# Rotary keys as the third column tile of w, and the early sums of w_out on ScalarE alone, in a hybrid attention block

## Chip, cores and metric

The kernel runs on one core of a Trainium2 chip. The metric is the device time in microseconds (us) of one execution; of the kernel before there are three timed runs and one more execution that was profiled. Engines are named TensorE (PE), VectorE (DVE), ScalarE (ACT), GpSimd (POOL) and SyncE (SP), as in the profile.

## The reference

One layer, 1024 tokens, width 1024, float32 in and out. One projection gives all heads; its columns are split among two head groups, and the result goes through the output projection and a layer norm:

```python
h = jnp.einsum('bsd,de->bse', x, w_in[layer])
q_a, k_a, v_a, z_a, q_b, k_b, v_b, z_b = jnp.split(h, SPLIT_POINTS, axis=-1)
y_a = neighborhood_attention(q_a..., k_a..., v_a..., rel_pos_bias[layer])   # 8 heads, 8 x 16 window of the grid
qb, kb = rotary(q_b..., positions), rotary(k_b..., positions)
y_b = windowed_gqa_with_sink(qb, kb, v_b..., sink_logits[layer])            # 8 query heads, 2 key heads
mixed = jnp.concatenate([y_a * silu(z_a), y_b * silu(z_b)], axis=-1)
y = jnp.einsum('bse,ed->bsd', mixed, w_out[layer])
x = layer_norm(DEEPNORM_ALPHA * x + y, ln_gain[layer], ln_bias[layer])
```

Rotary rotates each head of q_b and k_b by an angle that depends on the token; the keys k_b have 2 heads of 64, which is 128 columns of `w_in` and so one column tile of the kernel.

## The kernel before, in words

**Numbers.** Every float32 operand of a matmul is split into a high and a low float16 half, scaled by a power of two, and a product is three matmuls (high x high, high x low, low x high). ScalarE makes the high halves, GpSimd or VectorE the low ones.

**Stages.** First the values v are projected (line 537). Then come the 21 column tiles of `w_in` without v, 128 columns each, in the order of the list `ORDER` (lines 30 and 31): `zb` and `z` are gates of the two groups, `kb` and `qb` the rotary keys and queries, `k` and `q` those of the neighbourhood attention. The first six (`NPRO`) run ahead of the attention; the other fifteen (`FILL`) are pumped, matmul by matmul, between the steps of the attention. The attention has 128 units, one a step, group b first. The output projection and the layer norm end the kernel.

**A column tile** (`project`, lines 411 to 435) has two halves of 512 tokens; each half is 24 matmuls of 512 columns into one of two PSUM banks called `ps_pj`. Before a third half may start, the bank of the half two before it must have been emptied (`new_group`, line 406). Emptying is `evac`'s work:

- A gate tile named in `ORDER[:3]` is emptied by one Silu on ScalarE (line 391). A later gate tile takes a Tanh on ScalarE (line 394) and then a product on VectorE (line 395).
- A rotary tile (`rope`, line 358) is emptied by one scaled copy on ScalarE (line 364). Ahead of the attention VectorE then does a shuffle, two multiplications with cos and sin and an addition (lines 365 to 368); ScalarE casts the high halves (line 300, two instructions), VectorE subtracts to get the low ones (line 306, two), and for keys GpSimd copies both to the other 64 partitions (line 347, four).

**What sets the order.** From line 620 on the order of each engine's instructions is that in which the program emits them. Ahead of the attention a counter of matmuls (`ran`, 48 a tile) rules: an operation can be put at a count (`at`), or some matmuls after the end of a half. For a rotary tile the shuffle comes 2, the multiplications 3 and the addition 4 matmuls after the half's end, the casts 28, the subtractions 32, the copies 32 and 36 (lines 328 to 370).

Each tile needs a scale of its own, taken from sums of |w|: two sums on ScalarE (`w_scan`, line 260), one small matmul over all partitions (line 266) and five small VectorE instructions (lines 267 to 271), put 18 matmuls into the second half of the tile two before. All of `FILL` shares one scale. Its fifteen sums (`sum_w`, line 749: 12 on ScalarE at line 755, 3 on VectorE) are spread over counts 14 to 210; each has its own load of 512 KB (`ws`, line 689) on SP's queue. The last two, sums 13 and 14, sit at count 194, and the small matmul that adds them up on TensorE stands at count 217 (line 770), 25 matmuls later. Sixteen small VectorE instructions follow it (lines 267 to 286).

SP's queue also holds the loads of w's halves (line 229), each of which waits until GpSimd has made the low half five before it (line 246, lines 254 and 255), and the stores of v (line 739). What stands behind a waiting load waits too.

**The attention's planner.** During the attention a planner (lines 147 to 221 and 1379 to 1468) counts what it has given to each engine (`due`), with costs written down by hand, against 1.88 us a step (`at_step`). Work with a fixed engine is popped from queues; work that is not urgent goes by `fill_in` to an engine whose account has room (`ROOM`) before the next step, and work marked "any" to whichever asks first among those in its `cost`. Such are the sums of |w_out|, 16 of them (`wo_scan`, line 964): ScalarE (line 968) or VectorE (line 970) adds up one 128 x 512 piece. Four are made before the attention, on ScalarE. Twelve are created at the steps of `SCAN_LD` (0, 2, 4, 6, 8, 10, 13 and so on), together with their loads; each runs when its load is in, some steps later. The load of a piece waits for the sum four before it. When all 16 are made, the scale of `w_out` is worked out (line 782) and its split begins.

Of the kernel before, what the change touches and what calls it, by code (L numbers as in the profile page):

```python
# [26 lines left out]
QSCALE = 2.0 ** -15  # L27
LTT, LPP, BH, ND, NA, NX, F1 = 1, 6, 9, 1, 1, 8, 0.2
NSPLIT, NP = 6, 2
ORDER = ["zb0", "z0", "zb1", "kb", "qb0", "z1", "qb1", "zb2", "qb2", "k0", "qb3", "zb3", "q0", "k1", "q1",  # L30
         "k2", "q2", "k3", "q3", "z2", "z3"]
NPRO = 6
NS = 21 - NPRO
NR = 5
FILL = ORDER[NPRO:]
FILL_AT = [0, 8, 17, 25, 33, 41, 49, 57, 66, 74, 82, 90, 98, 106, 113, 121, 123.5, 126, 128, 131, 136]
# [29 lines left out]
def hybrid_block(ctx, tc, xT, x, wt, wv, wo, bias, sink, gain, lbias, cos, sin, bmask, out):  # L66
# [33 lines left out]
    def zslot(name, tag="z"):  # L100
        return zp.tile([128, S], F32, tag=tag, name=name, bufs=3 if tag == "z" else 1)
# [15 lines left out]
    invt = const.tile([128, 2], F32, name="invt")  # L117
    NT = len(ORDER)
    unit = const.tile([128, 2], F32, name="unit")
# [29 lines left out]
    clock = {"step": None}  # L149
# [19 lines left out]
    def enq(eng, fn, *deps, prio=1, after=0, cost=None):  # L169
        op = Op(eng, fn, deps, prio, cost)  # L170
        if clock["step"] is not None:
            queues[eng].append(op)
        elif after:
            events.setdefault(ran[0] + after, []).append(op.emit)
        else:
            op.emit()
        return op
# [44 lines left out]

    NH = 2 * len(ORDER)
    NL = NH - 2 * NR
# [37 lines left out]
    def w_scale(n):  # L262
# [8 lines left out]
        nc.vector.tensor_scalar(v, g, xrs, 0.5, op0=ALU.mult, op1=ALU.mult)  # L271
        nk, nq = ORDER.index("kb"), ORDER.index("qb0")
        if n >= NPRO - 1:
# [44 lines left out]
    def split_q(p, half, src, dep=None):  # L318
        col = dep is None
        ops, high = [], []  # L320
        prio = 0 if dep is None else 1
        eng = "pool" if dep and clock["step"] is not None else "dve"
        for j in range(2):
            a, o = slice(64 * j, 64 * j + 64), slice(64 - 64 * j, 128 - 64 * j)
            hi, lo = split_hl(lambda j=j, a=a: place(own("q", p, j), a, half, col),
                              lambda j=j, o=o: place(own("q", p, j), o, half, col),
                              taken_from(src, a, col), dep is None, eng)
            high.append((enq("act", hi, dep, prio=prio, after=28 if dep else 0), lo))
        for j, (o1, lo) in enumerate(high):
            ops.append(enq(eng, lo, *([o1] if dep else [h[0] for h in high]), prio=prio, after=32 if dep else 0))  # L330
            stk_ops.setdefault((p, j, half), []).append(ops[-1])
        return ops

    def split_k(p, half, src, dep=None):
        col = dep is None
        ops, high = [], []
        prio = 0 if dep is None else 1
        eng = "pool" if dep and clock["step"] is not None else "dve"
        for j in range(2):
            a, o = slice(64 * j, 64 * j + 64), slice(64 - 64 * j, 128 - 64 * j)  # L340
            hi, lo = split_hl(lambda j=j, a=a: place(own("kh", p, j), a, half, col),
                              lambda j=j, a=a: place(own("kl", p, j), a, half, col),
                              taken_from(src, a, col), dep is None, eng)

            def dup_(w, j=j, a=a, o=o):
                t = own(w, p, j)
                nc.gpsimd.tensor_copy(place(t, o, half, col), place(t, a, half, col))  # L347

            high.append((enq("act", hi, dep, prio=prio, after=28 if dep else 0), lo, dup_))
        for j, (o1, lo, dup_) in enumerate(high):  # L350
            o2 = enq(eng, lo, *([o1] if dep else [h[0] for h in high]), prio=prio, after=32 if dep else 0)
            ops.append(o2)
            dup = [enq("pool", lambda d=dup_: d("kh"), o1, after=32 if dep else 0, cost=0.62),
                   enq("pool", lambda d=dup_: d("kl"), o2, after=36 if dep else 0, cost=0.62)]
            stk_ops.setdefault((p, j, half), []).extend(dup)
        return ops

    def rope(ps, half):
        live = clock["step"] is not None
        sl = slice(512 * half, 512 * half + 512)  # L360
        eng, mul = ("pool", nc.gpsimd) if live else ("dve", nc.vector)
        raw = tiles["ap"].tile([128, 1024], F32, tag="va", name="rp_raw", bufs=6)[:, :512]
        sw = tiles["ap"].tile([128, 1024], F32, tag="va", name="rp_sw", bufs=6)[:, :512]
        o1 = enq("act", lambda: nc.scalar.activation(raw, ps, AF.Copy, scale=QSCALE), prio=0)
        o2 = enq("dve", lambda: nc.vector.stream_shuffle(sw, raw, SWAP), o1, after=2)
        o3 = enq(eng, lambda: mul.tensor_mul(raw, raw, tiles["cos"][:, sl]), o2, after=3)
        o4 = enq(eng, lambda: mul.tensor_mul(sw, sw, tiles["sin"][:, sl]), o2, after=3)
        o5 = enq(eng, lambda: mul.tensor_add(raw, raw, sw), o3, o4, after=4)
        return raw, o1, o5

    def evac(name, half, ps):
        sl = slice(512 * half, 512 * half + 512)
        kind = name.rstrip("0123")
        p = int(name[-1]) if name[-1].isdigit() else 0
        n = ORDER.index(name)
        if kind in ("kb", "qb"):
            raw, o1, o5 = rope(ps, half)
            if kind == "kb":
                split_k("b", half, raw, o5)
            else:  # L380
                split_q(f"b{p}", half, raw, o5)
            return [o1]
        if kind == "k":
            return split_k(p, half, ps)
        if kind == "q":
            return split_q(p, half, ps)
        e = 4 + p if kind == "zb" else p
        if half == 0:
            zt[e] = zslot(f"z{e}", ZTAG.get(name, "z"))
        if name in ORDER[:3]:  # L390
            nc.scalar.activation(zt[e][:, sl], ps, AF.Silu, scale=inv[:, n:n + 1])
            return []
        half_inv = invt[:, 0:1] if n < NPRO else invt[:, 1:2]
        o = enq("act", lambda: nc.scalar.activation(zt[e][:, sl], ps, AF.Tanh, scale=half_inv), prio=0)
        o2 = enq("dve", lambda: nc.vector.scalar_tensor_tensor(  # L395
            zt[e][:, sl], zt[e][:, sl], 1.0, ps, op0=ALU.add, op1=ALU.mult), o, prio=0)
        stk_ops.setdefault(name, []).append(o2)
        return [o2]
# [565 lines left out]
    def wo_scan(i, b):  # L964
        def scan(eng):
            m = wom[:, 4 * i + b:4 * i + b + 1]
            if eng == "act":
                nc.scalar.activation(junk2, wor[:, b], AF.Abs, accum_out=m)
            else:
                nc.vector.tensor_reduce(m, wor[:, b], axis=mybir.AxisListType.X, op=ALU.add, apply_absolute_value=True)  # L970

        scans.append(enq("any", scan, load_ops["wor", i, b], prio=1.9,
                         cost={"act": 0.85, "dve": 0.68} if clock["step"] is not None else {"act": 0.85}))

    for n in range(NSCAN):
        at(190 + 6 * n, wo_load, SCAN[n // 4], n % 4)
        at(222 + 8 * n, wo_scan, SCAN[n // 4], n % 4)
# [401 lines left out]
    for i in range(-LD, NU + LO):  # L1379
# [9 lines left out]
        if i in SCAN_LD:  # L1389
            n, b = divmod(NSCAN + SCAN_LD.index(i), 4)  # L1390
            wo_load(SCAN[n], b, *scans[-4:-3])
            wo_scan(SCAN[n], b)
# [7 lines left out]
        if i in B_LD:  # L1400
            n = B_LD.index(i)
# [145 lines left out]
```

## Time and profile before

| what | us |
| --- | --- |
| three timed runs | 445.05, 446.61, 447.45 (median 446.61) |
| the profiled execution's own time | 444.73 |
| its span, first to last instruction | 442.9 |
| what lies around the span | 1.83 |

| engine | busy us | share of the span |
| --- | --- | --- |
| TensorE, matmuls | 431.9 | 97% |
| VectorE | 333.6 | 75% |
| ScalarE | 313.7 | 71% |
| GpSimd | 280.5 | 63% |

A row of the timeline has the start in us from the beginning of the span, the time it took, engine, line, operation, output<-inputs and shapes, and how many instructions were merged into it; in brackets stands the idle time before it and who ended it. Matmuls overlap, so the time that one costs is the distance from its start to the next one's, not its own length. In the view of waits a row has who waited for whom, the sum in us, how often, and the longest. In the view of stretches a row has the stretch, its length and each engine's busy time in it.

### The profile page before, as it was taken

To read this page: it belongs to the slowest core of one execution; us is meant where nothing else is said; L and a number is where in the kernel's file an instruction comes from. 1 tells how busy PE (TensorE), PEld (TensorE's weight loads), DVE (VectorE), ACT (ScalarE), POOL (GpSimd) and SP (SyncE) were. 2 spreads that over 40 slices of the span, in tenths; PEclk is the share of its full clock that TensorE was granted. 3 is DMA by queue.
4 is the path that set the end of the run, shared out by engine and by line. 5 is a ranking of instruction groups with operands and counts; after the bars stand their busy time and mean duration, and the time that the engine had idled before them with its cause. 6 is when DMAs were issued, how large, how long until landed. Compare 5 with 4: busy or idle time off the path is not lost.

```text
span 442.9 us, 9338 instructions
## 1 busy us (share of the span) xinstructions
PE 431.9 (97%) x3205; PEld 251.3 (57%) x3205; DVE 333.6 (75%) x821; ACT 313.7 (71%) x660; POOL 280.5 (63%) x299
## 2 busy tenths in 40 slices
PE   8999999999999999999999999999999999999992
PEld 7997754444445555565555565656556565444451
DVE  5978967519988898888888977878778756665554
ACT  5749789759678888888988969788788753342221
POOL 0120074535848647779998799798989871077681
PEclk9999999999999999999999999999999999999997
DMA  7922469995138999985969999999799979612122
GB/s 255 406 95 60 132 234 337 259 308 161 48 96 184 188 195 186 206 162 123 179 137 214 194 198 210 225 185 187 141 199 228 154 130 385 252 47 96 47 91 100
DMA packets 128815, 80.12 MB, mean 181 GB/s; under 512 B 97280, under 2 KB 106368, under 8 KB 128768
## 3 DMA queue, kind: packets, MB, share of 16 engines
q1 hardware_dynamic: 128624, 79.40, 74.5%
q8 instruction: 25, 0.41, 0.4%
q14 instruction: 22, 0.18, 0.1%
q10 hardware_dynamic: 144, 0.13, 0.1%
HBM read 48.01 MB, written 8.42 MB: 127 GB/s over the span
## 4 chain that ended last, share of the span: by engine, by line
PE 80%; DMA 6%; DVE 5%; issue 3%; POOL 2%; ACT 1%; SPq 1%; POOLq 0%; DVEq 0%; ACTq 0%
PE ps_pj L430 35%; PE ps_s L1178 9%; PE ps_t L925 7%; PE ps_s L537 6%; PE ps_pj L1178 4%; PE ps_s L860 4%; PE ps_s L861 4%; DMA vd<-vt 3%; PE ps_pj L537 3%; PE ps_t L537 3%; PE ps_t L1178 2%; DMA ws<-in_wt 2%; PE ps_t L948 2%; POOL wl L246 1%; DMA wvraw<-in_wv 1%
## 5 line engine op out<-in xcount | busy, mean ns | idle before, releaser
L430 PE MATMUL ps_pj<-xf,wh 128*128 128x512 f16 x672 | 201.3, 379 | 1.1 <-DVE z L395 1.1
L430 PE MATMUL ps_pj<-xf,wl 128*128 128x512 f16 x336 | 127.3, 379 | 0.0
L430 PEld LDWEIGHTS <-wh 128*128 128x128 f16 x672 | 63.7, 98 | 61.0 <-issue 1.3
L885 ACT ACTIVATE ps_s<-sn,nm 128x385 f32<-128x385 f32 (+3 forms) x128 | 70.9, 554 | 32.5 <-DVE nm L870 32.2
L896 DVE SCALAR_TENSOR_TENSOR split<-ps_s,split 128x384 f16<-128x384 f32 (+1 forms) x128 | 66.8, 522 | 19.3 <-ACT split L895 17.7
L245 POOL TENSOR_SCALAR wr<-wr,wsc 128x512 f32<-128x512 f32 x32 | 23.8, 744 | 65.2 <-ACT wh L240 56.1
L895 ACT ACTIVATE split<-ps_s 128x384 f16<-128x384 f32 (+1 forms) x128 | 58.2, 454 | 1.6
L430 PEld LDWEIGHTS <-wl 128*128 128x128 f16 x336 | 32.8, 98 | 38.1
L870 DVE CUSTOM_DVE_ANT_0 sn<-ps_s,bias,sg 128x368 f32<-128x368 f32 (+1 forms) x64 | 36.2, 566 | 13.8 <-PE ps_s L861 13.8
L870 DVE CUSTOM_DVE_ANT_0 sn<-ps_s,bm,nsk 128x384 f32<-128x384 f32 (+1 forms) x64 | 40.7, 636 | 2.4 <-PE ps_s L861 2.2
L246 POOL TENSOR_TENSOR wl<-wr,wh 128x512 f16<-128x512 f32 x32 | 39.6, 1238 | 2.7
L860 PE MATMUL ps_s<-ks,qs 128*128 128x384 f16 (+2 forms) x128 | 39.7, 310 | 0.0
L861 PE MATMUL ps_s<-ks,qs 128*128 128x384 f16 (+2 forms) x128 | 39.7, 310 | 0.0
L925 PEld LDWEIGHTS <-tr 128*128 128x128 f16 (+1 forms) x1056 | 36.2, 98 | 2.4
L1178 PEld LDWEIGHTS <-A 128*128 128x128 f16 x216 | 20.1, 98 | 20.7
L347 POOL COPY ks<-ks 64x512 f16<-64x512 f16 x40 | 26.5, 662 | 5.8 <-DVE ks L306 1.8
L1213 DVE SCALAR_TENSOR_TENSOR xr<-ps_s,yc,xr 128x512 f32<-128x512 f32 (+1 forms) x22 | 16.0, 727 | 14.5 <-PE ps_s L1178 14.0
L1281 ACT ACTIVATE xr<-xr,nmr,rstd 128x1024 f32<-128x1024 f32 x6 | 7.4, 1240 | 27.0 <-POOL nmr L1232 27.0
L240 ACT ACTIVATE wh<-wr,wsc 128x512 f16<-128x512 f32 x32 | 22.8, 712 | 0.7 <-DVE wsc L270 0.7
L1178 PEld LDWEIGHTS <-m 128*128 128x128 f16 x144 | 13.9, 98 | 15.8
L537 PEld LDWEIGHTS <-xf 128*128 128x128 f16 x192 | 18.6, 98 | 7.2
L1283 POOL TENSOR_TENSOR xr<-xr,gb 128x512 f32<-128x512 f32 x13 | 16.8, 1290 | 8.3 <-ACT xr L1281 8.1
(214 smaller groups left out, 892.3 us busy)
## 6 DMA issues: line engine op xcount, KB each, us to landing
wr<-in_wt SPq DMA_DIRECT2D x32, 256.0 KB, 3.6
ws<-in_wt SPq DMA_DIRECT2D x15, 512.0 KB, 7.2
wor<-in_wo SPq DMA_DIRECT2D x20, 256.0 KB, 3.8
xr<-in_x SPq DMA_DIRECT2D x8, 512.0 KB, 10.6
out<-xr SPq DMA_DIRECT2D x15, 256.0 KB, 2.0
wob<-in_wo SPq DMA_DIRECT2D x14, 256.0 KB, 3.8
bias<-in_bias SPq DMA_DIRECT2D x8, 440.0 KB, 4.4
wvraw<-in_wv SPq DMA_DIRECT2D x9, 320.0 KB, 5.7
```

The lines of the kernel that those rows point to most:

```text
L246: nc.gpsimd.tensor_sub(l, raw, h)
L347: nc.gpsimd.tensor_copy(place(t, o, half, col), place(t, a, half, col))
L430: nc.tensor.matmul(ps, a[:, k % 4, :], mv, start=(k == 0 and i == 0), stop=(k == KT - 1 and i == 2))
L537: nc.tensor.matmul(ps[:, :320], lh[:, ts], rh[:, cs], start=(k == ko[0] and i == 0), stop=(k == ko[-1] and i == 2))
L860: nc.tensor.matmul(ps[:, :n], q, sl[0], start=True, stop=False)
L861: nc.tensor.matmul(ps[:, :n], q, sl[1], start=False, stop=True)
L870: nc.vector.tensor_tensor_reduce(sn[:, :n], ps[:, :n], bias_t, sg[:, c:c + 1], init, op0=ALU.add, op1=ALU.min, accum_out=nm)
L885: nc.scalar.activation(pt[:, :m], sn[:, :m], AF.Exp, bias=nm, scale=-1.0, accum_out=acc)
L895: nc.scalar.activation(hl[:, :m, 0, :], src, AF.Copy, scale=PSCALE)
L896: nc.vector.scalar_tensor_tensor(hl[:, :m, 1, :], src, PSCALE, hl[:, :m, 0, :], op0=ALU.mult, op1=ALU.subtract)
L925: nc.tensor.matmul(ps[:, w * m:w * m + e], a, b_, start=(i == 0), stop=(i == len(mms) - 1))
L1178: nc.tensor.matmul(ps[:, cs], lh[:, 128 * t:128 * t + 128], rh[:, cs], start=(fresh and e == 0 and n == 0), stop=(e == len(terms) - 1 and ...
```

## The change

Two edits. In `ORDER` the tiles `kb` and `zb1` change places: the rotary keys become the third tile and the gate `zb1` the fourth. So that `zb1` is still emptied by a Silu, the test for the first three names becomes a test for the first four places (a rotary tile never comes to that line). The host lays out the columns of `w_in` by `ORDER`, so loads and matmuls stay the same in number, size and order. Second, a sum of |w_out| that is created at step 4 of the attention or before may go to ScalarE alone; before, only those made ahead of the attention were bound to it.

```diff
-ORDER = ["zb0", "z0", "zb1", "kb", "qb0", "z1", "qb1", "zb2", "qb2", "k0", "qb3", "zb3", "q0", "k1", "q1",
+ORDER = ["zb0", "z0", "kb", "zb1", "qb0", "z1", "qb1", "zb2", "qb2", "k0", "qb3", "zb3", "q0", "k1", "q1",
          "k2", "q2", "k3", "q3", "z2", "z3"]
...
-        if name in ORDER[:3]:
+        if n < 4:
             nc.scalar.activation(zt[e][:, sl], ps, AF.Silu, scale=inv[:, n:n + 1])
             return []
...
         scans.append(enq("any", scan, load_ops["wor", i, b], prio=1.9,
-                         cost={"act": 0.85, "dve": 0.68} if clock["step"] is not None else {"act": 0.85}))
+                         cost={"act": 0.85, "dve": 0.68} if (clock["step"] or 0) > 4 else {"act": 0.85}))
```

## The prediction

> **What bounds the kernel now.** First the page: how full is TensorE?
>
> ```profile
> span 442.9 us, 9338 instructions
> ...
> PE 431.9 (97%) x3205; PEld 251.3 (57%) x3205; DVE 333.6 (75%) x821; ACT 313.7 (71%) x660; POOL 280.5 (63%) x299
> ```
>
> TensorE is without a matmul for 11 us of 442.9 (442.9 - 431.9). The waits of TensorE say where it waited for somebody:
>
> ```profile
> PE ps_t L1250 <- ACT dr L1248: 2.7, 1, 2.7
> PE ps_pj L430 <- DVE z L395: 1.1, 1, 1.1
> PE ps_t L463 <- DVE warm L132: 1.0, 1, 1.0
> PE ps_pj L537 <- ACT wvh L493: 0.7, 1, 0.7
> ```
>
> L1250 belongs to the last rows' norm, L463 and L537 to the first loads; the change touches none of them. One is left: a matmul of a column tile that waits for VectorE's product L395. The stretch behind it, from 123.5 us to 423 us:
>
> ```profile
> 123.50:423.00 299.50, 299.48 (x2410) 165.43 (x2410) 230.62 (x606) 219.03 (x483) 224.98 (x232) 1.00 0.83 176
> ```
>
> The first figure after the length is TensorE: 299.48 of 299.50 us. The attention and the output projection are one unbroken run of matmuls at the full granted clock (the 1.00). Work moved about on VectorE or ScalarE in there can cost time, but has none to win. So **the whole prize is the one gap**; here it is in TensorE's timeline, with VectorE's behind it:
>
> ```profile
> 122.04 0.27 PE L860 MATMUL ps_s<-ks,qs 128*128 128x256 f16 x1
> 122.15 0.27 PE L861 MATMUL ps_s<-ks,qs 128*128 128x256 f16 x1
> 123.52 0.59 PE L430 MATMUL ps_pj<-xf,wh 128*128 128x512 f16 x2 [1.10 <-DVE z L395]
> ```
>
> ```profile
> 107.79 1.81 DVE L306 TENSOR_TENSOR ks<-rp_raw,ks 64x512 f16<-64x512 f32 x2
> 109.63 0.17 DVE L267 TENSOR_REDUCE wg<-ps_t 128x1 f32<-128x15 f32 x1
> ...
> 111.97 0.73 DVE L365 STREAM_SHUFFLE rp_sw<-rp_raw 128x512 f32<-128x512 f32 x1
> ...
> 115.39 1.40 DVE L306 TENSOR_TENSOR ks<-rp_raw,ks 64x512 f16<-64x512 f32 x2
> ...
> 116.82 0.73 DVE L365 STREAM_SHUFFLE rp_sw<-rp_raw 128x512 f32<-128x512 f32 x1
> ...
> 120.12 2.63 DVE L306 TENSOR_TENSOR qs<-rp_raw,qs 64x512 f16<-64x512 f32 x2
> 122.78 0.69 DVE L395 SCALAR_TENSOR_TENSOR z<-z,ps_pj 128x512 f32<-128x512 f32 x1
> ```
>
> A matmul of 256 columns takes 0.11 us from start to start (122.04 to 122.15), so the seventh tile could start at 122.26; it starts at 123.52: **1.26 us lost** (the view of waits, which counts from the modelled end, says 1.10). It needs the bank of z1's first half, which L395 empties at 123.47, last in a queue on VectorE without a hole: subtractions for the keys (ks), the scale's small instructions, the queries' rotation, more ks, more rotation, the queries' subtractions (qs). 22 us earlier the same engine has nothing to do:
>
> ```profile
> 90.46 0.20 DVE L271 TENSOR_SCALAR inv<-wg,unit 128x1 f32<-128x1 f32 x1
> 99.02 0.01 DVE L365 LOAD_MASK_SELECT rp_sw<-rp_raw  x1 [8.35 <-ACT rp_raw L364]
> ```
>
> **First edit: keys third.** TensorE's matmuls are the same, so the time changes only through gaps. ScalarE shows where halves end and what it does:
>
> ```profile
> 85.90 0.69 ACT L391 ACTIVATE z<-ps_pj,inv 128x512 f32<-128x512 f32 x1 [1.37 <-PE ps_pj L430]
> ...
> 95.98 1.06 ACT L755 ACTIVATE junk<-ws 128x1024 bf16<-128x1024 f32 x1 [3.58 <-DMA ws<-in_wt]
> ...
> 98.40 0.57 ACT L364 ACTIVATE rp_raw<-ps_pj 128x512 f32<-128x512 f32 x1
> ...
> 101.86 0.58 ACT L364 ACTIVATE rp_raw<-ps_pj 128x512 f32<-128x512 f32 x1
> 103.14 0.72 ACT L240 ACTIVATE wh<-wr,wsc 128x512 f16<-128x512 f32 x1 [0.70 <-DVE wsc L270]
> 103.76 1.04 ACT L755 ACTIVATE junk<-ws 128x1024 bf16<-128x1024 f32 x1
> ...
> 105.89 0.19 ACT L755 ACTIVATION_READ_ACCUMULATOR junk<-ws 128x1 f32 x1
> 105.99 1.24 ACT L300 CAST ks<-rp_raw 64x512 f16<-64x512 f32 x2
> ...
> 118.03 0.67 ACT L394 ACTIVATE z<-ps_pj,invt 128x512 f32<-128x512 f32 x1
> ```
>
> *What leaves the crowded place.* The third tile's first half ends at 85.9 (the Silu there waited for it), so the keys' shuffle, products and subtractions move from 99 to 116 us into 86 to 102, most of it into the 8.35 us hole. After the scale's matmul at 106.69 (row below) VectorE then has only: small instructions 2.34 us (109.63 to 111.97), first rotation 3.42 (111.97 to 115.39), second 3.30 (116.82 to 120.12), qs 2.63. From 106.9 that ends at 118.6. Its input, the Tanh, ends by 118.70 even in its old place. So L395 ends near 119.4, 2.9 us before 122.26: the 1.26 us go, and it would take 2.9 us of new lateness to bring any of it back. What is late next is the Tanh of z1's second half, whose bank is wanted a half tile later; it costs nothing.
>
> *What arrives elsewhere.* On ScalarE, between 95.98 and the last sum of w, two copies (0.57 + 0.58) become two Silus (0.69 each): +0.23. The keys' casts were two pairs behind that sum; the first now falls at 92, into the 3.58 us wait for a load; the second, 28 matmuls after 91.1, falls ahead of the sum: +1.24. The wait of 0.70 for the scale (wsc) goes, since VectorE is free: -0.70. So the last two sums, 13 and 14, now from 103.76 to 106.08 (105.89 + 0.19), shift by 0.77: from 104.53 to 106.85. Who waits for it?
>
> ```profile
> 106.69 0.17 PE L266 MATMUL ps_t<-wm,ones 128*128 128x15 bf16 x1
> ```
>
> TensorE itself, in its queue: with 0.61 us to spare before, late by **0.16** after. The bounds are 0 (each end of that sum is read to some tenths) and 0.8: each casts' pair and Silu could also hit a wait for a load. I take 0.16, as every term is a measured row.
>
> *At nothing:* the keys' four GpSimd copies per half come into GpSimd's own waits; SP's loads keep their order. If that cover fails, GpSimd's low halves of w slip, SP's loads behind them too, and then the sums: that is rival 1.
>
> [...] The keys' products would now meet GpSimd's low halves. The rows for it:
>
> ```profile
> 92.50 0.69 POOL L245 TENSOR_SCALAR wr<-wr,wsc 128x512 f32<-128x512 f32 x1 [2.35 <-ACT wh L240]
> ...
> 118.03 1.52 POOL L245 TENSOR_SCALAR wr<-wr,wsc 128x512 f32<-128x512 f32 x1
> ```
>
> Alone 0.69 us, beside VectorE's rotation 1.52: a loss of 0.83 a meeting. [...]
>
> **Second edit: early sums of w_out.** Followed by hand through the planner's account, only the sums created at steps 0, 2 and 4 change, two of which went to VectorE (at steps 11 and 12):
>
> ```profile
> 143.15 0.68 DVE L970 TENSOR_REDUCE wom<-wor 128x1 f32<-128x512 f32 x1
> ...
> 144.80 0.68 DVE L970 TENSOR_REDUCE wom<-wor 128x1 f32<-128x512 f32 x1
> ```
>
> ScalarE's account has room at steps 12 (booked to 23.66; the limit is the next step's 24.44 less `ROOM`'s 0.35), 14 and 16, so they go there, one after the other; the sum created at step 8 finds ScalarE full at 18 and goes to VectorE at 19. From step 21 both accounts are as before; no load moves, nor the scale behind the sums. Net: VectorE loses one sum, ScalarE gains one, and near 144 us VectorE is freed of 1.4 us (2 x 0.68) where it is fullest:
>
> ```profile
> 140.00:150.00 10.00, 10.00 (x81) 5.46 (x79) 9.50 (x27) 8.93 (x24) 8.87 (x8) 1.00 0.89 180
> ```
>
> VectorE 9.50 of 10, ScalarE 8.93, TensorE full. TensorE now arrives 1.1 us sooner, and VectorE is the one that could fail to follow; the edit gives it more than that. I cost it at 0: TensorE's run covers it. If the cover is gone it costs at most ScalarE's extra sum (about 0.7, as VectorE's); gain below nothing is excluded, as no TensorE idle is there to win.
>
> **Sum, against the profiled execution.** -1.26 + 0.16 = -1.10. Span 442.9 - 1.1 = 441.8; with the 1.83 around it 443.6 instead of 444.73. The median of the runs shown, 446.61, lies 1.88 above the profiled one; carried over, **445.5 us**, 0.25% less.
>
> **Rivals.**
>
> 1. *The sums of w become the wait (slower).* The mechanism: two blocked GpSimd halves or late loads push sums 13 and 14, hence L266. Break-even: the last sum ends 1.1 us after my 106.85, at 107.95. For it: the loads are issued behind loads of w that wait for GpSimd, and the last lands just before it is used:
>
> ```profile
> 94.46 0.34 SPq L229 DMA_DIRECT2D wr<-in_wt  x1
> 94.85 0.43 SPq L689 DMA_DIRECT2D ws<-in_wt  x1
> ```
>
> ```profile
> 94.85 8.62 DMA ws<-in_wt
> ```
>
> It landed at 103.47; sum 13 would start at 104.53, so 1.06 us are to spare. Against: it takes 0.83 four times (3.3 us) to land at 106.8, end the sums 2.3 us later at 109.1 and stall TensorE 2.4 us: net -1.26 + 2.4 = +1.1, 447.7 us. Chance 0.12 for this side of the break-even.
>
> 2. *The gap is only moved.* TensorE comes 1.1 us sooner, and somewhere past 140 us VectorE, ScalarE or a transpose isn't ready; the next gap returns the gain: 446.6. For it: 9.50 of 10 above. Against: those engines begin sooner too, as VectorE's queue ends at 123.5 no more. Chance 0.13.
>
> 3. *VectorE holds GpSimd up, twice.* Two meetings (2 x 0.83 = 1.66 us) put the load at 105.13, sum 13 another 0.6 us late: net -1.10 + 0.6 = -0.5, 446.1. For it: the 1.52 above; against: GpSimd's two low halves before the load need not both meet a product. Chance 0.10. [...]
>
> 4. *The second edit does nothing*, because the queues differ from what I followed: then the time is that of the first edit alone, 445.5 or rival 2's.
>
> **How the numbers follow.** Forecast (445.5, from 445.3 with no wait at L266 to 446.2 with 0.8): 0.60. The last 0.05 is for a gain larger than the gap: the runs shown are 0.3 to 2.7 us above the profiled one, so they may hold gaps that it lacks, and the change may close one (444.0). Runs differ by 2.4 us, about 0.5%, which is what a measurement here can tell from no change; that bound is 2.2 us, 444.4 or 448.8. Forecast and rivals 2 to 4 lie inside; below 444.4 come the last case and the lower runs of the forecast, 0.15; above 448.8 part of rival 1, 0.08; within, 0.77. Range: from 443.9 (445.5 less the runs' 1.6) to 447.8, just past rival 1's price.
>
> **What would show it.** Right: no wait of TensorE for L395; rp_raw at 85.9 and 91.1; VectorE's hole at 91 to 99 filled; L395 of z1's first half done before 120; L266 of 15 columns started within 0.3 us of 106.7; no L970 before 148 us; TensorE still whole from 122.3 to 422. Wrong: any wait of TensorE for L755, a new one for L896 or a transpose after 140 us, or a wait for the scale of the fifth tile.

## The result, and the profile after

| | before | change |
| --- | --- | --- |
| median, us (11 runs each) | 446.11 | 443.28 |
| lowest and highest, us | 444.57, 447.48 | 441.67, 444.78 |
| profiled execution and its span, us | 444.73, 442.9 | 443.17, 441.4 |

The ratio is 0.9942 (95% interval 0.9923 to 0.9960): the change makes the kernel **2.6 us faster** (0.58%; 1.8 to 3.4 by the interval), where 1.1 us was forecast. The time lies below the range of the prediction. Of the miss of 2.2 us (445.5 forecast), 0.5 us is the base: the forecast stood on the median of three runs, 446.61, and that of eleven is 446.11. One execution is left out of all numbers below, the profiled one of the experiment "Silu, and two instructions more" (762 us at a granted clock of 0.56), from whose trace therefore no start time is used.

The forecast came from TensorE's gaps, so those come first. TensorE's waits in the changed kernel (who waited for whom, us in total, times, longest):

```profile
PE ps_t L1250 <- ACT dr L1248: 3.0, 1, 3.0
PE ps_t L463 <- DVE warm L132: 1.0, 1, 1.0
PE ps_pj L537 <- ACT wvh L493: 0.3, 1, 0.3
PE ps_pj L537 <- DVE x L515: 0.3, 1, 0.3
```

The wait for L395 is gone, and this view lists no new one in the attention. TensorE's timeline around the place of the gap, and the two stretches by engine:

```profile
122.12 0.27 PE L860 MATMUL ps_s<-ks,qs 128*128 128x256 f16 x1
122.23 0.27 PE L861 MATMUL ps_s<-ks,qs 128*128 128x256 f16 x1
122.34 0.38 PE L430 MATMUL ps_pj<-xf,wh 128*128 128x512 f16 x1
```

```profile
123.50:423.00 299.50, 299.35 (x2410) 165.33 (x2409) 229.93 (x604) 220.41 (x486) 225.38 (x232) 1.00 0.82 175
140.00:150.00 10.00, 10.00 (x81) 5.49 (x80) 8.59 (x24) 8.90 (x25) 7.51 (x8) 1.00 1.07 190
```

The seventh tile's matmul starts 0.11 us behind its neighbour, where it started 1.37 us behind it before. So the 1.26 us are won, as forecast, and the stretch behind it is as full as before but for 0.15 us. That cannot make 2.6 us. The rest lies behind TensorE's last matmul of the projection, at the very end. ScalarE's last rows, before and after ("ACTq" is a row of ScalarE's queue that is not counted as busy; here it hands the last store to the DMA queue):

```profile
437.75 0.37 ACT L1253 COPY xr<-ps_t 128x256 f32<-128x256 f32 x1 [1.32 <-PE ps_t L1251]
438.15 2.05 ACTq L1257 DMA_DIRECT2D out<-xr  x1
```

```profile
437.87 0.37 ACT L1253 COPY xr<-ps_t 128x256 f32<-128x256 f32 x1 [1.99 <-PE ps_t L1251]
438.27 0.37 ACTq L1257 DMA_DIRECT2D out<-xr  x1
```

The same store of 128 KB takes 2.05 us to issue before and 0.37 us after: **1.68 us**. From issue to landing (last figure of the view of DMA issues) it is, before and after:

```profile
out<-xr ACTq DMA_DIRECT2D x1, 128.0 KB, 3.5
```

```profile
out<-xr ACTq DMA_DIRECT2D x1, 128.0 KB, 1.8
```

Nothing comes behind that store but the end of the kernel, so its 1.7 us are on the path. 1.26 + 1.68 = 2.94 us, against 2.6 us by the ratio and 2.83 us by the two medians.

There is one smaller difference at the end. From TensorE's last matmul to the end of the span it is 5.57 us before and 3.60 us after: 1.96 us less, of which the issue is 1.68; the other 0.28 us is the copy L1253, which starts 0.37 us behind that matmul before and 0.09 us after. The changed kernel loses the same 0.28 us a little earlier, where TensorE waits 3.0 us in place of 2.7 for L1248, so the sum of 2.94 stands. In both kernels it is row number 831 of ScalarE that starts late, 0.34 to 0.35 us behind the semaphore row ahead of it; the same two instructions follow their semaphore rows in 0.06 us in the other kernel, where they have other numbers. What makes that row late was not tried.

The two profiled executions differ by only 1.56 us. The one of the change came to the gap 0.08 us later, lost 0.33 us from start to start at a short wait at 240 us, and happened to pay 0.94 us for TensorE's clock at the end:

```profile
435.73 1.19 PE L1250 MATMUL ps_t<-xr,dr 128*128 128x256 f32 x2 [2.99 <-ACT dr L1248]
436.71 1.06 PE L1251 MATMUL ps_t<-gb,dn 128*128 128x256 f32 x2
```

From the start of L1250 to the end of L1251 these are 2.04 us; before it was 1.10 us (436.27 to 437.37). The clock that the profile grants had fallen to half in the idle time before L1250 (at 435.39 us; before, at 437.70). Of the 12 undisturbed traces of this study without the experiment on that clock, 4 show 1.10 us and 8 show 1.37 to 2.05 us, and both lengths occur among kernels with the long issue and among those with the short one; what decides the moment of the fall was not found.

What makes an issue take 2.05 us was not known at this point. The experiments went a wrong way first and came back to it.

### The profile page after: what moved, and what is told of

It is laid out like the page before. It is cut to its first block, busy times and chain, and to the rows that moved or that the text cites. A ratio compares the mean times of both kernels' runs of the same rounds, so it can differ in the third digit from the quotient of the medians.

```text
span 441.4 us, 9341 instructions
## 1 busy us (share of the span) xinstructions
PE 433.0 (98%) x3205; PEld 252.2 (57%) x3205; DVE 334.7 (76%) x820; ACT 314.3 (71%) x662; POOL 279.2 (63%) x299
## 4 chain that ended last, share of the span: by engine, by line
PE 94%; DMA 2%; DVE 2%; SPq 0%; ACT 0%; issue 0%; DVEq 0%; ACTq 0%
PE ps_pj L430 49%; PE ps_s L1178 9%; PE ps_t L925 7%; PE ps_s L537 6%; PE ps_pj L1178 4%; PE ps_s L860 4%; PE ps_s L861 4%; PE ps_pj L537 3%; PE ps_t L537 3%; PE ps_t L1178 2%; PE ps_t L948 2%; DMA wvraw<-in_wv 1%; DMA tr<-split 1%; DVE stats L1219 1%; DVE xr L1213 1%; DVE xr L1278 0%
## 5 line engine op out<-in xcount | busy, mean ns | idle before, releaser
L246 POOL TENSOR_TENSOR wl<-wr,wh 128x512 f16<-128x512 f32 x32 | 40.3, 1258 | 2.7
L1178 PEld LDWEIGHTS <-A 128*128 128x128 f16 x216 | 20.1, 98 | 20.7
L347 POOL COPY ks<-ks 64x512 f16<-64x512 f16 x40 | 25.5, 638 | 4.5 <-ACT ks L298 1.8
L1178 PEld LDWEIGHTS <-m 128*128 128x128 f16 x144 | 13.9, 98 | 15.8
```

The lines of the kernel that those rows point to most:

```text
L246: nc.gpsimd.tensor_sub(l, raw, h)
L1178: nc.tensor.matmul(ps[:, cs], lh[:, 128 * t:128 * t + 128], rh[:, cs], start=(fresh and e == 0 and n == 0), stop=(e == len(terms) - 1 and ...
```

## The experiments

Ratios are to the kernel before on the same chip, with the 95% interval.

**Theory A (the forecast's):** the gap is all there is to win. **Theory B (the reserve):** VectorE follows TensorE with little to spare between 150 and 290 us, and anything that lets VectorE run ahead wins there. **The code load** was formed only after the eighth run (the "theory C" in the third text below is another): the length of ScalarE's instruction stream decides where a load of its instructions falls, and before the change it fell on the last issue.

### Keys alone

The kernel before with the first two hunks of the diff only.

> The first edit alone: keys third, the early sums of w_out free to go to VectorE as before. Theory A (the forecast's: the gap of 1.26 us at z1's bank is all, only its size is other in the timed runs) expects the whole gain of the change here, a ratio of 0.994 to before, and no wait of TensorE for L395. Theory B (the second edit frees VectorE near 144 us and so removes waits of TensorE that the timed runs have and the profiled one lacked) expects only the gap here, 0.997 (-1.1 to -1.3 us), and new waits of TensorE after 140 us in this trace.

Measured: 442.19 us, **0.9929** (0.9909 to 0.9949). All of the change's gain comes with the first edit alone, as theory A asked. The 0.997 and the new waits that theory B asked for are not there: TensorE waits only for L1250 and L463.

### Sums alone

The kernel before with the last hunk of the diff only.

> The second edit alone: keys fourth as before, the early sums of w_out on ScalarE. Theory A expects 1.000 (within 0.5 us) and the wait of TensorE for L395 near 122 us still there with 1.1 us. Theory B expects 0.996 to 0.997 (-1.3 to -1.7 us) with that wait still there, as what was saved lies elsewhere.

Measured: 443.87 us, **0.997** (0.9955 to 0.9986), faster by 1.3 us with the gap still in place:

```profile
122.49 0.27 PE L861 MATMUL ps_s<-ks,qs 128*128 128x256 f16 x1
124.18 0.59 PE L430 MATMUL ps_pj<-xf,wh 128*128 128x512 f16 x2 [1.42 <-DVE z L395]
```

So theory A falls: there is something to win besides the gap for L395. Also, 0.71% and 0.3% do not add up to the change's 0.58%.

### The gap closed in another way

Keys stay fourth and the sums as they were; the product L395 for z1 goes, since one Silu on ScalarE empties its bank.

```diff
-        if name in ORDER[:3]:
+        if name in ORDER[:3] or name == "z1":
...
-        i = 0 if e in (4, 0, 5) else 1 if e == 1 else 2
+        i = 0 if e in (4, 0, 5, 1) else 2
```

> Before, but the gate tile z1, the last ahead of the attention, is emptied by one Silu on ScalarE instead of a Tanh there and a product on VectorE; the keys stay fourth and the sums as before. VectorE has no hand in the bank that the seventh tile waits for. Theory A expects no wait near 122 us and the same gain as the change, 0.994. Theory B expects -1.1 to -1.3 us, 0.997. A third theory C (moving the keys gains by itself something besides that gap, as a wait at another place of the first 123 us) expects this kernel at 0.997 and the keys alone at 0.994.

Measured: 444.48 us, **0.9984** (0.9967 to 1.0002). The wait for L395 is gone; two small ones have come:

```profile
PE ps_s L860 <- DVE split L896: 0.4, 2, 0.3
...
PE ps_t L948 <- DVE on L937: 0.2, 1, 0.2
```

The gap alone is worth 0.7 us here (0 to 1.5). Theory A's 0.994 falls here too, and the third theory of the text, that moving the keys gains something besides the gap, comes nearest; what that something is was found later. The two new waits suggested theory B.

### The change once more

> The changed kernel once more, beside the other three on the same chip: 0.994 if the first measurement holds, and a second trace of it. All theories expect no wait of TensorE between 60 and 240 us; the first trace's 0.3 us at 240 us, behind a transpose, may or may not come back.

Measured: 442.81 us, **0.9942** (0.9923 to 0.9961), on the chip of the three runs above; the gain has come again. The short wait at 240 us has not; in its place one of 0.5 us has come at 271 us, again for a transpose, and the stretch from 123.5 to 423 us holds 298.95 us of matmuls:

```profile
PE ps_t L925 <- DMA tr<-split: 0.5, 1, 0.5
```

Such a wait comes in the kernel before too (0.3 us in its third trace, below), so it speaks for none of the theories.

### Silu and sums together

> z1 emptied by a Silu (no gap at 122 us) and the early sums of w_out on ScalarE, the keys fourth as before. The theory now (reserve): beside the one gap, before loses some more in runs of its own at places past 150 us where VectorE's split or a transpose is ready only 0.4 to 0.7 us ahead of TensorE; whatever gives VectorE a lead there wins the rest, and z1's Silu alone, which lets TensorE come 1.26 us sooner without giving VectorE a lead, gave part of it back as waits at 180 to 189 us. It expects here the whole gain without moving the keys: 0.994 to 0.995 and no wait of TensorE for L896 or L937. Rival (the place of the keys gains by itself): no better than z1's Silu alone, 0.998.

Measured: 442.56 us, **0.9945** (0.9924 to 0.9965), and no waits but those for L1250 and L463. The sums that brought 0.3% alone bring 0.4% on top of the Silu. That was what theory B asked for; it is also what an independent second gain gives, wherever it lies.

### The lead taken away

The change, with one more reduction of 128 x 1024 on VectorE at the first step of the attention.

```diff
+        if i == 0:
+            nc.vector.tensor_reduce(spare, tiles["cos"], axis=mybir.AxisListType.X, op=ALU.max)
```

> The changed kernel with one extra instruction on VectorE at the first step of the attention, a maximum over the cosine table, 128 x 1024, whose result nobody uses (about 1.2 us, as the sums L757 of that shape). It takes from VectorE the lead that the moved keys gave, without a wait of TensorE at 122 us. The theory of the reserve expects the time to rise by 0.5 to 1.3 us over the change (0.996 to 0.997 to before) and TensorE to wait for L896, L937 or transposes between 150 and 290 us by about that much in all. The forecast's reading (a run without holes covers what VectorE does) expects 0.994, as the change.

Measured: 442.89 us, **0.9962** (0.9947 to 0.9977). The shift from 0.9942 is within the intervals, and TensorE's waits in the trace are the two old ones:

```profile
PE ps_t L1251 <- ACT dr L1249: 3.0, 1, 3.0
PE ps_t L464 <- DVE warm L133: 1.0, 1, 1.0
```

Inconclusive: the ratio is one that theory B named, but a taken lead showed no stall of the 0.5 to 1.3 us that should make it.

### Two more looks at the kernel before

Each is one execution with a profile.

> The kernel before once more, for a second trace of it. The theory of the reserve expects the wait for L395 at 122 us with 1.1 us or more and besides it waits for L896, L937 or transposes past 150 us that the first trace hadn't, in all 0.5 to 1.5 us. The theory that the gap itself is larger expects 2 to 2.5 us at 122 us and nothing behind it.

> The kernel before a third time, with the same expectations as the second trace: how much the waits at 122 us and past 150 us differ from run to run.

Measured: 445.63 and 444.38 us. The waits of the first:

```profile
PE ps_t L1250 <- ACT dr L1248: 2.7, 1, 2.7
PE ps_pj L430 <- DVE z L395: 1.3, 1, 1.3
PE ps_t L463 <- DVE warm L132: 1.0, 1, 1.0
```

The second has 1.1 us for L395 and only one wait that the first trace of this kernel hadn't, 0.3 us for a transpose. Theory B has no place left to put its 1.3 us. So the spans were cut into pieces, and the piece that followed the kernels, not chance, was the last issue. For each undisturbed trace: the row number of L1257 among all rows of ScalarE (counted from 0, queue rows included), its duration, the number of rows that ScalarE had started when the trace's records of DMA queue 14, of the kind "instruction", show the last load of 8 KB within the span, and the time from the issue's start to the end of the span. The last three rows belong to the experiments below.

```
kernel                      row   issue us   load at row   issue to end us
before                      833   2.05       834           4.79
before, look 1              833   2.44       834           5.19
before, look 2              833   2.18       834           4.93
Silu for z1                 833   1.92       834           4.66
sums alone                  835   0.37       832           3.58
keys alone                  835   0.37       832           3.11
Silu and sums               835   0.37       832           3.12
change                      837   0.37       834           3.11
change again                837   0.37       833           3.12
lead taken                  837   0.37       834           3.32
before, two more            835   0.37       832           3.09
change, four fewer          833   1.89       834           4.64
change, kept warm           837   0.37       833           3.57
```

The load comes at row 832 to 834 of ScalarE in every kernel: one block of its instructions seems to end there, and the next 8 KB to be loaded (the traces show the loads, not the blocks). Where L1257 is row 833, it stands at that edge: the load starts 0.3 to 0.9 us into the issue, and the issue ends 1.1 to 1.2 us behind the load's end. Where ScalarE has two or four rows more, the edge comes before the issue, and the load runs during ScalarE's last small operand (L1249) and the 1.0 us or more that it then waits for TensorE ahead of L1253; there the issue stays at 0.37 us. Where the rows come from can be read too. A sum on ScalarE is two rows (at line 968 the sum, 0.61 to 0.63 us, and the reading of its accumulator, 0.19 us). For the keys alone it is this, in the answer for line 300:

```profile
L300 ACT CAST ks<-rp_raw x4: 605/610/616, 92.9 to 99.9; 64x512 f16<-64x512 f32 x4
L300 ACTq EVENT_SEMAPHORE  x2: 38/38/38, 90.9 to 91.0; - x2
```

In their new place the keys' casts have two semaphore instructions of their own, 38 ns each, which the kernel before has not. Two rows, and the edge is off the last issue. That is also why the gains of the two edits do not add up: each of them takes away the same long issue.

The page of the profile has two queues of the kind "instruction", with the same figures before and after the change (packets, MB, share of 16 engines):

```profile
q8 instruction: 25, 0.41, 0.4%
q14 instruction: 22, 0.18, 0.1%
```

0.41 MB / 25 is 16 KB a packet; 0.18 MB / 22 is 8 KB, the size of the load in the table. That the last load in queue 14 is ScalarE's is shown by the next experiment: with two rows more on ScalarE and nothing else changed it comes 2.6 us behind TensorE's last matmul ahead of its idle time at the end, where it came 5.1 us behind it (434.56 less 431.94, 438.65 less 433.56).

### Two instructions more in the kernel before

Two of the eight scalings of the residual rows are cut in halves, near 395 us, where ScalarE has time (busy 3.32 of the 10 us from 390 to 400).

```diff
-            nc.scalar.activation(xrs[t], xrs[t], AF.Copy, scale=ALPHA)
+            for h in (slice(0, 512), slice(512, 1024)) if t in (3, 6) else (slice(0, 1024),):
+                nc.scalar.activation(xrs[t][:, h], xrs[t][:, h], AF.Copy, scale=ALPHA)
```

> The kernel before, with two scalings of the residual rows (L1208, rows 6 and 3, at about 395 us) cut into two halves each: ScalarE has two instructions more, nothing else changes, and VectorE's work stays. Theory of the code load: at the end of the kernel before, ScalarE's issue of the last store (L1257, the 833rd of its rows in the trace) takes 2.05 to 2.44 us, and in three traces of that kernel and the one of the Silu a load of 8 KB of instructions falls into just that issue; with 835 or 837 rows ahead it is 0.37 us and the load comes earlier, in an idle stretch. Then this kernel is 1.7 us faster (ratio 0.996, as the sums alone), the issue takes 0.37 us, and the gap of 1.3 us for L395 is still there. Theory of VectorE's lead: nothing changes, ratio 1.000.

Measured: 442.74 us, **0.9966** (0.9945 to 0.9986). A kernel with *more* work is 1.5 us faster. Its last issue, and TensorE's wait for the bank of z1:

```profile
436.68 0.37 ACTq L1258 DMA_DIRECT2D out<-xr  x1
```

```profile
PE ps_pj L430 <- DVE z L395: 0.4, 1, 0.4
```

The wait is still there, though in this execution it is 0.4 us, not 1.3. Theory B, which asked for 1.000, falls.

### Silu, and two instructions more

> The kernel with z1 emptied by one Silu (it gave 0.9984), with the same two scalings cut in halves; the sums stay as before. Code load: it comes to what Silu and sums gave together, 0.9945 (0.993 to 0.996), with the last issue at 0.37 us. VectorE's lead: it stays at 0.998, since VectorE does as many sums as before.

Measured: 442.72 us, **0.9957** (0.9938 to 0.9977). It moves from the Silu's 0.9984 towards the 0.9945 of Silu and sums, with the sums untouched; the interval just about excludes the 0.998 of theory B. The last issue took 0.37 us.

### Four instructions fewer in the change

Four of the scalings go from ScalarE to VectorE; L1257 (here L1260) is row 833 again.

```diff
-            nc.scalar.activation(xrs[t], xrs[t], AF.Copy, scale=ALPHA)
+            if t in (2, 3, 6, 7):
+                nc.vector.tensor_scalar_mul(xrs[t], xrs[t], ALPHA)
+            else:
+                nc.scalar.activation(xrs[t], xrs[t], AF.Copy, scale=ALPHA)
```

> The changed kernel, with four of the eight scalings L1208 (rows 2, 3, 6 and 7, from 378 us on) on VectorE in place of ScalarE: ScalarE has four instructions fewer, so L1257 is its 833rd row again. Code load: the last issue takes 2 us again and the time goes up by 1.7 us: ratio to the kernel before 0.998 in place of 0.9942, with no gap at 122 us. VectorE's lead: nothing of the attention is touched, 0.994. If VectorE's four scalings delay a bank in the output projection, the waits of TensorE after 378 us show it.

Measured: 443.99 us, **0.999** (0.997 to 1.0009): the gain of the change is all but gone, though the gap at 122 us is closed. The waits of TensorE and the last issue:

```profile
PE ps_t L1253 <- ACT dr L1251: 2.7, 1, 2.7
PE ps_t L463 <- DVE warm L132: 1.0, 1, 1.0
PE ps_pj L537 <- ACT wvh L514: 0.3, 1, 0.3
```

```profile
437.61 1.89 ACTq L1260 DMA_DIRECT2D out<-xr  x1
```

No bank of the output projection is late, so the four scalings on VectorE cost nothing there; what came back is the long issue. With the two runs before it the effect is shown in both directions: two rows more take it away, four rows fewer bring it back.

### The clock kept up at the end

The change, with 40 matmuls into an unused half bank ahead of the last rows' statistics.

```diff
+            for _ in range(40):
+                nc.tensor.matmul(pn[:, 256:384], warm, warm, start=True, stop=True, skip_group_check=True)
```

> The changed kernel, with 40 matmuls of 128 columns into the unused half of the last bank, right ahead of the last rows' statistics, for nothing but to keep TensorE from idling there: in the traces of the change, of the keys alone and of Silu and sums the granted clock fell to 0.5 some 3.4 to 3.8 us after the last matmul of the projection, and L1250 to L1251 took 1.75 to 2.05 us, against 1.10 us in those where it fell later. If the clock is worth that, this kernel is up to 0.9 us faster than the change: ratio 0.992 to 0.994, L1250 to L1251 in 1.10 us. If it is not, 0.9942 as the change.

Measured: 442.14 us, **0.9951** (0.9934 to 0.9968). (The 3.4 to 3.8 us of the text count from the start of the projection's last matmul, L1178; two more matmuls, L1243, follow it ahead of the idle time.)

```profile
431.01 2.40 PE L1245 MATMUL ps_t<-warm 128*128 128x128 f16 x40
434.15 0.67 PE L1252 MATMUL ps_t<-xr,dr 128*128 128x256 f32 x2 [0.74 <-ACT dr L1250]
434.66 0.59 PE L1253 MATMUL ps_t<-gb,dn 128*128 128x256 f32 x2
```

The clock stays up (434.15 to 435.25 are 1.10 us), and in this trace the span is 439.3 us. The ratio is no better than the change's 0.9942, so a gain of up to 0.9 us is neither shown nor excluded. No kernel here beats the change by more than the intervals; the keys alone (0.9929) come out level with it.

## Why the prediction was wrong

The place and the mechanism of the first edit were right, and the sum of its gaps was about right. What failed is the step ahead of it, "**the whole prize** is the one gap", which rests on "TensorE's matmuls are the same, so the time changes only through gaps". That holds up to TensorE's last matmul. Behind it this kernel has 5.6 us more (442.94 less 437.37), in which the last copy is made and its store issued and landed, and its timeline showed an issue of 2.05 us there that the prediction did not read and so put at nothing. With it falls "gain below nothing is excluded, as no TensorE idle is there to win" for the second edit: that edit alone gave 0.3% by its one sum more on ScalarE, which was counted correctly and priced at nothing. Nor is the first edit only a move of work, as the prediction took it: it adds two semaphore rows to ScalarE, which shift the last issue off the load (keys alone, 2.05 to 0.37 us).

Point by point:

- **The gap, -1.26.** Gone, as forecast. Over whole executions its worth comes out at 0.4 us (change with four fewer, 0.999) to 0.7 us (Silu, 0.9984) where the issue is long. Where it is short, it comes out at 0.4 us (Silu and two more against before and two more, 0.9957 and 0.9966) to 1.8 us (keys alone against sums alone, 0.9929 and 0.997). The gap itself is 0.4 to 1.4 us by the waits of the single executions. No closer figure is to be had with intervals of 0.2% each way.
- **The margin of 2.9 us at L395.** It was 0.9 us: L395 ended at 121.45, not 119.4. VectorE's rows of the changed kernel:

```profile
110.70 0.68 DVE L367 TENSOR_TENSOR rp_sw<-rp_sw,sin 128x512 f32<-128x512 f32 x1
...
113.89 0.01 DVE L365 LOAD_MASK_SELECT rp_sw<-rp_raw  x1 [1.78 <-ACT rp_raw L364]
...
115.71 1.64 DVE L367 TENSOR_TENSOR rp_sw<-rp_sw,sin 128x512 f32<-128x512 f32 x1
...
118.48 2.25 DVE L306 TENSOR_TENSOR qs<-rp_raw,qs 64x512 f16<-64x512 f32 x2
120.76 0.69 DVE L395 SCALAR_TENSOR_TENSOR z<-z,ps_pj 128x512 f32<-128x512 f32 x1
```

  The second rotation waited for ScalarE, which stood behind the first sums of w_out and their load, and then ran beside GpSimd (1.64 us for a product that takes 0.68 us at 110.70):

```profile
111.81 0.63 ACT L968 ACTIVATE junk<-wor 128x512 bf16<-128x512 f32 x1 [3.38 <-DMA wor<-in_wo]
...
113.27 0.58 ACT L364 ACTIVATE rp_raw<-ps_pj 128x512 f32<-128x512 f32 x1
```

  GpSimd's row in that place:

```profile
115.33 1.47 POOL L246 TENSOR_TENSOR wl<-wr,wh 128x512 f16<-128x512 f32 x1
```

  The prediction let VectorE run on without asking when ScalarE would hand over the second half. The margin was wide enough all the same.
- **The sums of w (rival 1), +0.16.** The last sum ended at 106.73 us (forecast 106.85), and L266 started at 106.78, within the 0.3 us named. It held TensorE up by 0.02 us in this trace, and by 0.19 us in the second trace of the change and in that of the keys alone, so the 0.16 was of the right size. (The sums stand 23 matmuls ahead of L266, 194 to 217, not 25.)

```profile
106.54 0.19 ACT L755 ACTIVATION_READ_ACCUMULATOR junk<-ws 128x1 f32 x1
```

```profile
106.78 0.17 PE L266 MATMUL ps_t<-wm,ones 128*128 128x15 bf16 x1
```

- **Where the keys went.** rp_raw came at 85.97 us, as forecast, and at 92.63, not 91.1, as ScalarE was then waiting for the load of a sum:

```profile
85.97 0.60 ACT L364 ACTIVATE rp_raw<-ps_pj 128x512 f32<-128x512 f32 x1 [1.37 <-PE ps_pj L430]
...
91.58 1.06 ACT L755 ACTIVATE junk<-ws 128x1024 bf16<-128x1024 f32 x1 [1.39 <-DMA ws<-in_wt]
...
92.63 0.58 ACT L364 ACTIVATE rp_raw<-ps_pj 128x512 f32<-128x512 f32 x1
```

  VectorE's hole was filled as described (busy 5.65 of the 8 us from 91 to 99, 0 before). The meeting with GpSimd that rival 3 is about took place, at 95 us, where VectorE's product took 1.63 us (0.68 us at 110.70) beside a row of GpSimd (L246, 94.69 to 96.16, 1.47 us; 1.16 us at 106.80); the sums were not late for it:

```profile
93.25 0.01 DVE L365 LOAD_MASK_SELECT rp_sw<-rp_raw  x1 [2.52 <-ACT rp_raw L364]
...
95.07 1.63 DVE L367 TENSOR_TENSOR rp_sw<-rp_sw,sin 128x512 f32<-128x512 f32 x1
```

- **The sums of w_out.** L970 went from 6 to 5 and L968 from 10 to 11, and the first L970 came at 148.4 us: the planner was followed rightly by hand. From the answer for line 970 (durations, first and last start):

```profile
L970 DVE TENSOR_REDUCE wom<-wor x5: 676/683/686, 148.4 to 172.3; 128x1 f32<-128x512 f32 x5
```

- **TensorE after 140 us** stayed whole but for 0.15 us of 299.50, and for 0.55 us in the second trace, so rival 2 came at most in part, and rivals 1 and 3 did not come. The last case, "a gain larger than the gap", did, though not by its reason: what was closed besides is no gap of TensorE.

## What to carry to other kernels

When a kernel is bound by one engine nearly throughout, read the last 10 us row by row as well, queue rows too: here all that followed that engine's last instruction was on the path (5.57 us before, 3.60 us after). If two builds differ by a microsecond or two that no wait explains, compare the number of instructions on each engine and the durations of the last issues, and try the same kernel with two idle instructions more: here the count set where a load of code fell, and a change that merely shifts the count can pass for a gain (two rows more in the kernel before: 0.9966) or a loss (four fewer in the change: 0.999 in place of 0.9942).

## What the runs showed of the hardware

- An issue that took 0.37 us in the eight traces of the table in which ScalarE had more rows took 1.89 to 2.44 us in the five where a load of 8 KB of instructions fell into it. It was shown for ScalarE's last issue alone; whether other loads in the middle of the kernel cost as much when no wait covers them was not tried.
- TensorE stood idle for 2.7 to 3.0 us ahead of its last four matmuls (0.7 us with the 40 small ones), and its granted clock fell to half 2.4 to 4.8 us after the idle time began. Where it fell ahead of these four or just at their start, they took 1.98 to 2.05 us; where it fell while they ran, 1.37 to 1.76 us; where it fell behind them, 1.10 us. The moment differs from trace to trace: in that of the change it was 2.65 us after the modelled end of the last matmul (432.74 to 435.39 us), in the first of the kernel before 4.14 us (433.56 to 437.70).
